# A hybrid decoder layer: later modulation moved from GpSimd to TensorE in four column strips, and the delta rule's heads taking turns

## The chip, the core and the metric

One Trainium2 chip, one core of it. A core has five engines that run at the same time and meet only through semaphores: TensorE (PE: matmuls; its weight loads are PEld), VectorE (DVE), ScalarE (ACT), GpSimd (POOL) and SyncE (SP). Each executes its own list of instructions in order. SP issues nearly all DMA transfers here, so a transfer that must wait for a buffer holds those behind it in SP's list. The metric is the device time of one execution in microseconds (us), as the median of several runs; less is better.

## What is computed

One decoder layer over 1,024 tokens of width 2,048, in float32. A conditioning vector c gives six modulation vectors; the tokens pass a mixer with four parallel head groups and then a mixture of experts, each with a DeepNorm residual:

```python
mod = (jax.nn.silu(c) @ w_ada[l] + b_ada[l]).astype(F32)
sh1, sc1, gt1, sh2, sc2, gt2 = jnp.split(mod, 6, axis=-1)
h = ada_input(x, sh1, sc1)
p = h @ w_in[l]
y_conv = short_conv_mixer(...)
y_rwkv = rwkv7_mixer(...)          # the delta rule, 8 heads of 64
y_att = swa_sink_attention(...)    # window 128, sinks, relative bias
y_ssm = s5_mixer(...)
y_mix = jnp.concatenate([...], axis=-1) @ w_out[l]
x = layer_norm(ALPHA * x + (1.0 + gt1) * y_mix, ln_g[l, 0], ln_b[l, 0])
h = ada_input(x, sh2, sc2)
y_moe = hierarchical_moe(h, ...)   # top-1 group, then top-2 of 8 experts
x = layer_norm(ALPHA * x + (1.0 + gt2) * y_moe, ln_g[l, 1], ln_b[l, 1])
```

The delta rule keeps a 64 x 64 state per head: `state = state * w + v k^T + (state a) b^T`, read out as `state r` at each token. The first two modulation vectors (sh1, sc1) are needed before anything else; the other four, 4 x 2,048 columns, only from the output projection on. They are the "later modulation": a product of a vector of 2,048 numbers with 2,048 x 8,192 weights, 64 MB that are read once.

## The kernel before

Stages, in order of time: the startup (layer norm of the first 512 tokens, sh1 and sc1, the first columns of the input projection); the mixers; the rest of the output projection with the router; the experts; the last layer norm.

**The mixers** are one program order made of two interleaved streams. The first is the chain of the mixers itself: for each half of 512 tokens four calls of `rw_core` (two heads each) and the attention, and after the first half the state-space part. This chain is long, with small steps on DVE, ACT and PE that wait for each other. The second stream, the fill (`fills`), is the large matmuls: the input projection unit by unit, then blocks `a` and `b` of the output projection. It is a Python generator that yields after each group of three matmuls (a product of 128 x 128 by 128 x 512, split into a high and a low part) the time that it is thought to take, `MM3` = 0.64. At places where the chain would leave PE waiting, it calls `hop(us)`, which pulls that many microseconds of fill. All PE instructions are kept in program order, so this decides PE's list. The lists of the other engines are ordered by the scheduler of the framework with a simulated time line. For each weight tile of the fill ACT makes the high part (L325) and DVE the low part (L326); both are read by PE a little later.

**Side work** stands in two lists, P and Q, of which `side()` takes one item each; `side` is called three times in `rw_core`, once per attention block and once per state-space group. P held the eight tables of the state-space part (POOL), and then 16 blocks of the later modulation, two items each. `mod_part` makes a block of 512 columns: 16 tiles of 128 x 512 are loaded into the ring `mw` of six buffers (L579), POOL multiplies each by its column of silu(c) (L580) and adds it to a running sum (L582), and `end` loads the bias, lets PE sum over the 128 partitions with a column of ones, adds the bias on DVE (L590) and writes the 512 numbers to `md_d` in device memory. The ring `mw` is also used by the tables, the convolution and the output blocks.

**`rw_core`** treats 512 tokens in 8 chunks of 64, for two heads at once (64 partitions each). A loop of 31 steps (`tv`, L758 and L759) inverts 32-row triangular blocks on DVE, with `hop(0.88)` in each step. Later `pa` multiplies the solved blocks of the even chunks (partitions 0 to 63) and of the odd ones (64 to 127), L812, into the two buffers of `rwB`, and L814 and L815 copy the results out. In the last loop each chunk has 8 matmuls: for head 0 and then for head 1 two into the output `py` and two into the new state `pS` (bank `rwS`); DVE scales `pS` into the state `St` (L841).

`bias_rows` (Q) loads the bucket table and multiplies it at once (bank `rwA`).

PSUM in this stage: four `acc` banks for the fill, one `rwA`, two `rwB`, one `rwS`.

Of the kernel before, what the change touches and what calls it, by code (L numbers as in the profile page):

```python
# [11 lines left out]
F32 = mybir.dt.float32  # L12
# [3 lines left out]
ALU = mybir.AluOpType  # L16
# [4 lines left out]
D = 2048  # L21
S = 1024
HT = 512
KT = D // 128
# [44 lines left out]
PT = {}  # L69
# [97 lines left out]
class K:  # L167
# [203 lines left out]
    def unit(s, ws, ui, half, nxt):  # L371

        u = UNITS[ui]
        s5 = u[0][0] == "s5"
        n = 4 if s5 else len(u)
        acc = [s.ps("acc") for _ in range(n)]
        k = 0
        while k < KT:
            hi, lo = next(ws)
            for kk in range(hi.shape[1]):  # L380
                hh, hl = s.hk(half, k)
                a = 0
                for j in range(n):
                    if s5:
                        sl = slice(128 * j, 128 * j + 128)
                        s.mm3(acc[j], (hh[:, sl], hl[:, sl]), (hi[:, kk], lo[:, kk]), k == 0, k == KT - 1)
                    else:
                        w = u[j][2]
                        s.mm3(acc[j][:w], (hi[:, kk, a:a + w], lo[:, kk, a:a + w]), (hh, hl), k == 0, k == KT - 1)
                        a += w  # L390
                    yield MM3
                k += 1
                s.turn(half, nxt, k)
        for j in range(n):
            if s5:
                t = s.ev()
                s.nc.scalar.copy(t, acc[j])
                r0 = HT * half + 128 * j
                s.nc.sync.dma_start(s.u_d[r0:r0 + 128], t)
            else:  # L400
                s.spill(u[j], acc[j], half)
# [168 lines left out]
            s.nbs += 1  # L570
        return rest

    def mod_part(s, ci):

        nc, io, E = s.nc, s.io, s.nc.gpsimd
        a = s.mt()
        for k in range(KT):
            w = s.mt()
            nc.sync.dma_start(w, io["w_ada"][128 * (KT * ci + k):128 * (KT * ci + k) + 128])  # L579
            E.tensor_tensor(w if k else a, w, s.cs[:, k:k + 1].to_broadcast([128, 512]), op=ALU.mult)  # L580
            if k:
                E.tensor_tensor(a, a, w, op=ALU.add)  # L582

        def end():
            o = D * 2 + 512 * ci
            b = s.ev()
            nc.sync.dma_start(b[0:1], io["b_ada"][0:1, o:o + 512])
            pm = s.ps("rwB")
            s.mm(pm[0:1], s.c["ones"][:, 0:1], a, start=True, stop=True)
            nc.vector.scalar_tensor_tensor(b[0:1], pm[0:1], 0.0 if ci // 4 == 1 else 1.0, b[0:1], op0=ALU.add, op1=ALU.add)  # L590
            nc.sync.dma_start(s.md_d[0:1, 512 * ci:512 * ci + 512], b[0:1])
        return end

    def mod(s, t, c0):

# [94 lines left out]
    def rw_core(s, u, follow):  # L690

        nc, c, V, E = s.nc, s.c, s.nc.vector, s.nc.gpsimd
# [52 lines left out]
        for ch in range(NCH):  # L745
            e = ch % 2
# [58 lines left out]
        s.hop(1.1)  # L805
        XA = s.t4().rearrange("p (e x t) -> p e x t", e=2, t=64)
        for g in range(NCH // 4):
            for e in range(2):
                pa = s.ps("rwB")
                for x in range(4):  # L810
                    ix = 4 * g + x
                    s.mm(pa[0:64, x * 128:x * 128 + 128], XT[64 * e:64 * e + 64, ix], G[64 * e:64 * e + 64, ix // 2, ix % 2], start=True, stop=True)  # L812
                pv = pa[0:64].rearrange("p (x a t) -> p x a t", x=4, a=2)
                nc.scalar.copy(XA[0:64, e, 4 * g:4 * g + 4], pv[:, :, 0])  # L814
                V.tensor_copy(WV[0:64, e, 4 * g:4 * g + 4], pv[:, :, 1])  # L815
        PT = s.t2().rearrange("p (c t) -> p c t", t=64)
# [12 lines left out]
        py = s.ps("rwA")  # L829
        St = s.St[hp]  # L830
        for ch in range(NCH):
            pS = s.ps("rwS", (128, 64))
            e = ch % 2
            for h in range(2):
                sl = slice(64 * h, 64 * h + 64)
                x = (ch // 2) * 2 + h
                s.mm(py[sl, ch * 64:ch * 64 + 64], WV[:, e, x], RB[:, e, x, 0:64], start=True, stop=False)
                s.mm(py[sl, ch * 64:ch * 64 + 64], St[sl], R[sl, ch], start=False, stop=True)
                s.mm(pS[sl], RB[:, e, x, 64:128], WV[:, e, x], start=True, stop=False)
                s.mm(pS[sl], PT[sl, ch], St[sl], start=False, stop=True)  # L840
            V.tensor_scalar(St, pS, DC[:, ch:ch + 1], None, op0=ALU.mult)  # L841
            s.step()
            s.hop(1.1)
# [57 lines left out]
    def bias_rows(s):  # L901
        nc = s.nc
        rb = s.ev()
        nc.sync.dma_start(rb[0:32, 0:8], s.io["rel_bias"])
        nc.gpsimd.memset(rb[32:33, 0:8], NEG)
        oh = s.ev()
        nc.sync.dma_start(oh[0:33, 0:384], s.io["oh"][0:33])
        pf = s.ps("rwA")
        s.mm(pf[0:8, 0:384], rb[0:33, 0:8], oh[0:33, 0:384], start=True, stop=True)
        f = s.ev()  # L910
        nc.vector.tensor_copy(f[0:8, 0:384], pf[0:8, 0:384])
        nc.sync.dma_start(s.F_d, f[0:8, 0:384])
        nc.sync.dma_start(s.F2_d, s.F_d[None].to_broadcast([128, 8, 384]))
# [418 lines left out]
    def startup_and_mix(s):  # L1332
# [6 lines left out]
        with tc.tile_pool(name="EV", bufs=1, side=s.R) as s.EV:  # L1339
            with tc.tile_pool(name="start", bufs=1, side=s.R) as P, tc.tile_pool(name="ps0", bufs=1, space=PSUM) as s.psum:  # L1340
                s.psb = {"acc": 6, "tp": 2}
                s.startup(P)
            s.np, s.n2, s.n4, s.n8 = 6, 9, 6, 2
            with tc.tile_pool(name="LO", bufs=1, side=s.R) as s.LO:
                mix = s.LO.tile([128, MIX.shape[1]], F32, name="mix")
                nc.sync.dma_start(mix, io["mix"])
                for k, (a, n) in MIX_AT.items():
                    s.c[k] = mix[:, a:a + n]
                with tc.tile_pool(name="s5p", bufs=1, side=s.R) as P5:
                    s.s5_params(P5, s.LO)  # L1350
                with tc.tile_pool(name="M", bufs=1, side=s.R) as s.M, tc.tile_pool(name="ps1", bufs=1, space=PSUM) as s.psum:
                    s.psb = {"acc": 4, "rwA": 1, "rwB": 2, "rwS": 1}
                    s.mixers()

    def mixers(s):
# [22 lines left out]
        for gb in range(8):  # L1378
            P.append(lambda gb=gb: (rests.pop(gb - 1)() if gb else 0, rests.update({gb: s.s5_tables(gb)})))
        P.append(lambda: rests.pop(7)())  # L1380
        for ci in range(16):
            P.append(lambda ci=ci: rests.update({"m": s.mod_part(ci)}))
            P.append(lambda: rests.pop("m")())
        for i in range(4, 8):
            Q.append(lambda i=i: rests.update({"n": s.norm_b(i)}))
            if i in (9,):
# [57 lines left out]
            s.side()  # L1444
        while s.fill:
            s.pump()
        while s.convs:
            s.conv(*s.convs.pop(0))
        s.pin = False
# [13 lines left out]
    def out_cols(s, ws, key, acc, js=range(4), nxt=None):  # L1463

        for k in range(KT):
# [7 lines left out]
                yield MM3  # L1473
            if nxt:
                s.turn(key, nxt, k + 1)

    def out_block(s, ws, key, n, nxt):

        nc, V = s.nc, s.nc.vector
        ns = slice(512 * n, 512 * n + 512)  # L1480
        g = s.mt()
        s.mod(g, 512 * n)
        acc = [s.ps("acc") for _ in range(4)]
# [675 lines left out]
```

## Time and profile before

| | |
|---|---|
| median of three runs | 3643.0 us (3624.75 to 3646.46) |
| the profiled execution | 3632.17 us, of which the profile's span is 3630.4 us |
| granted TensorE clock over the span | 0.93 of full speed |
| PE busy | 3157.3 us, 87% of the span |
| DVE / ACT / POOL busy | 2632.2 / 1601.3 / 1443.0 us |

By stage, from the span's start: the startup to about 130 us; the mixers, with the tables on POOL from about 200 to 630 us and the later modulation on POOL from about 630 to 1880 us; output projection and router to about 2210 us; the experts to about 3530 us; then the last layer norm.

Times of one kind of instruction are given as busy time (overlaps counted once) and as the mean of one in nanoseconds. Matmuls overlap in the pipeline, so what one costs is better read from the distance between starts than from its length. A matmul of full float32 shows as two records, one of the split products as one. The granted clock is a share of full speed, averaged over the stretch; the two levels are 1.2 and 2.4 GHz. The columns of a stretch are its bounds, its length, then for each engine its busy time and instructions.

### The profile page before, as it was taken

How to read it: one execution, taken by the hardware profiler on the slowest of the kernel's cores; microseconds unless marked ns; L12 is line 12 of the kernel's file. 1: busy time of each engine (PE TensorE's matmuls, PEld its weight loads, DVE VectorE, ACT ScalarE, POOL GpSimd, SP SyncE). 2: the span in 40 equal slices, each digit the busy share in tenths (PEclk: the TensorE clock that was granted, in tenths of full speed). 3: DMA queues.
4: the chain of work that ended last, by engine and by line, in shares of the span. 5: the costliest groups of instructions: out<-in, count | busy, mean ns of one | idle time of the engine just before them, and what ended most of it. 6: DMA issues, size and time to landing. Idle time of an engine off the chain costs nothing. (4 is left out here: it accounts for less than half of the span.)

```text
span 3630.4 us, 46775 instructions
## 1 busy us (share of the span) xinstructions
PE 3157.3 (87%) x15757; PEld 2330.7 (64%) x15757; DVE 2632.2 (73%) x3973; ACT 1601.3 (44%) x2316; POOL 1443.0 (40%) x1173
## 2 busy tenths in 40 slices
PE   6888989888998998998888876998998999999980
PEld 4666767655577676666657664776776766667750
DVE  2466758595576468678556987698797796896986
ACT  4332323222322332322323545576675675675751
POOL 0067574677787004444444542042142151340411
PEclk9999989899999999899999967999999999999995
DMA  9555444564787445545446657799798897997964
GB/s 360 190 161 154 127 144 149 166 197 144 221 262 221 143 115 168 166 144 161 149 143 233 209 216 284 250 367 355 261 395 322 290 388 276 328 389 259 370 248 186
DMA packets 345301, 844.94 MB, mean 233 GB/s; under 512 B 93251, under 2 KB 173164, under 8 KB 280908
## 3 DMA queue, kind: packets, MB, share of 16 engines
q1 hardware_dynamic: 336396, 808.11, 63.4%
q0 software_dynamic: 8640, 33.61, 3.7%
q8 instruction: 129, 2.11, 0.2%
q14 instruction: 136, 1.11, 0.1%
HBM read 754.72 MB, written 111.49 MB: 239 GB/s over the span
## 5 line engine op out<-in xcount | busy, mean ns | idle before, releaser
L1841 DVE TENSOR_TENSOR partl<-raw,parth 128x1024 fp32r<-128x1024 f32 x768 | 903.9, 1221 | 160.4 <-ACT parth L1840 158.2
L1840 ACT CAST parth<-raw 128x1024 fp32r<-128x1024 f32 x768 | 776.5, 1049 | 283.8 <-PE h L180 151.6
L326 DVE TENSOR_TENSOR wlo<-wraw,whi 128x512 fp32r<-128x512 f32 (+2 forms) x472 | 417.0, 888 | 291.3 <-ACT whi L325 281.5
L325 ACT CAST whi<-wraw 128x512 fp32r<-128x512 f32 (+2 forms) x472 | 283.0, 603 | 729.0 <-PE acc L180 613.2
L580 POOL TENSOR_TENSOR mw<-mw,cs 128x512 f32<-128x512 f32 x256 | 305.6, 1200 | 603.2 <-DMA mw<-in_w_ada 296.4
L1922 POOL DMA_INDIRECT sum_d<-yo,list x37 | 253.3, 6846 | 624.6 <-DVE yo L1920 582.2
L180 PE MATMUL h<-partl,xh 128*128 128x512 f32 x1184 | 479.5, 409 | 9.4 <-DVE partl L1841 8.1
L180 PE MATMUL h<-parth,xh 128*128 128x512 f32 x1184 | 456.3, 399 | 12.7 <-ACT parth L1840 12.7
L180 PE MATMUL acc<-hh,whi 128*128 128x512 f32 (+1 forms) x1056 | 447.5, 428 | 15.3 <-ACT hh L352 7.0
L180 PE MATMUL acc<-hh,wlo 128*128 128x512 f32 (+1 forms) x1056 | 424.9, 404 | 40.8 <-DVE wlo L326 40.7
L180 PE MATMUL acc<-hl,whi 128*128 128x512 f32 (+1 forms) x1056 | 423.0, 401 | 0.0
L582 POOL TENSOR_TENSOR mw<-mw 128x512 f32<-128x512 f32 x240 | 347.8, 1449 | 6.4
L180 PE MATMUL acc<-whi,hh 128*128 128x512 f32 x640 | 274.0, 447 | 32.5 <-DVE ev L1490 18.3
L180 PE MATMUL acc<-wlo,hh 128*128 128x512 f32 x640 | 269.4, 421 | 33.6 <-DVE wlo L326 32.2
L180 PEld LDWEIGHTS h<-partl,xh 128*128 128x128 f32 x1184 | 225.8, 191 | 93.8 <-DVE partl L1841 48.2
L180 PEld LDWEIGHTS acc<-hh,wlo 128*128 128x128 f32 (+1 forms) x1056 | 202.7, 192 | 98.2 <-DVE wlo L326 51.5
L180 PEld LDWEIGHTS h<-parth,xh 128*128 128x128 f32 x1184 | 225.7, 191 | 61.2 <-ACT parth L1840 18.4
L180 PE MATMUL acc<-whi,hl 128*128 128x512 f32 x640 | 264.4, 413 | 0.0
L180 PEld LDWEIGHTS acc<-hh,whi 128*128 128x128 f32 (+1 forms) x1056 | 202.4, 192 | 84.1 <-issue 24.1
L1940 POOL DMA_INDIRECT xg<-h_d,list x39 | 114.0, 2923 | 348.1 <-DMA list<-list_d 224.2
L180 PE MATMUL y<-parth,al 128*64 128x512 f32 (+1 forms) x592 | 233.5, 399 | 14.3 <-DVE al L1901 7.9
L180 PE MATMUL y<-partl,ah 128*64 128x512 f32 (+1 forms) x592 | 237.1, 401 | 9.2 <-DVE partl L1841 9.2
(441 smaller groups left out, 5337.6 us busy)
## 6 DMA issues: line engine op xcount, KB each, us to landing
raw<-in_moe_w SPq DMA_DIRECT2D x384, 1024.0 KB
mw<-in_w_ada SPq DMA_DIRECT2D x256, 256.0 KB
wraw<-in_w_in SPq DMA_DIRECT2D x240, 256.0 KB
wraw<-in_w_out SPq DMA_DIRECT2D x160, 256.0 KB
wa<-in_wa SPq DMA_DIRECT2D x32, 1024.0 KB
pT_d<-ev SPq DMA_DIRECT2D x62, 256.0 KB
t<-s_tab SPq DMA_DIRECT2D x24, 512.0 KB
s_tab<-mw SPq DMA_DIRECT2D x32, 256.0 KB
```

The costliest lines, as they stand in the source:

```text
L180: return s.pinned(s.nc.tensor.matmul(*a, **k))
L325: s.nc.scalar.copy(v(hi), v(raw))
L326: s.nc.vector.tensor_sub(v(lo), v(raw), v(hi).bitcast(F32))
L580: E.tensor_tensor(w if k else a, w, s.cs[:, k:k + 1].to_broadcast([128, 512]), op=ALU.mult)
L582: E.tensor_tensor(a, a, w, op=ALU.add)
L1840: nc.scalar.copy(hi, x)
L1841: nc.vector.tensor_sub(lo, x, hi.bitcast(F32))
L1922: nc.gpsimd.indirect_dma_start(out=s.sum_d, out_offset=bass.IndirectOffsetOnAxis(ap=lst[0:n, 0:1].bitcast(I32), axis=0), in_=o, in_offset= ...
L1940: nc.gpsimd.indirect_dma_start(out=s.xgs[x][0:n], out_offset=None, in_=s.h2_d, in_offset=bass.IndirectOffsetOnAxis(ap=l[0:n, 0:1].bitcast( ...
```

## The change

1. **Later modulation.** `mod_part` goes, and with it POOL's multiplications and additions and the products with a column of ones. `mod_parts` is a generator of 64 steps (16 blocks of 512 columns, four steps each). A step takes four weight tiles of 128 x 512 and cuts each into four pieces of 128 columns; piece j is multiplied by the same column of silu(c), repeated 32 times as the weights, into strip j of 32 partitions of `rwS[:, 128:256]`. Every fourth step adds the bias by four matmuls with one row. DVE collects each step's result from PSUM (`mdacc`), and after the fourth writes four rows of 128 to `md_d`. The loads of the next step, and the bias, are issued right after the matmuls of this one. `modstep` runs one step; `unit` and `out_cols` call it after each four k, as fill worth 0.9, and an output block first runs what it needs.
2. **The heads take turns.** In each chunk the new state comes first, and each of the four kinds of matmul is issued for head 0 and head 1 before the next kind.
3. **Even and odd solved blocks take turns** in `pa`; both results are copied out after a `hop(0.88)`.
4. **`bias_rows`** has a `hop(8.8)` between its loads and its matmul.
5. `rwS` is one tile for the whole stage: columns 0 to 63 for the state, 128 to 255 for the modulation.

```diff
@@ unit
                 s.turn(half, nxt, k)
+                if k % 4 == 0 and s.mdp:
+                    yield s.modstep()
@@
-    def mod_part(s, ci):
-        nc, io, E = s.nc, s.io, s.nc.gpsimd
-        a = s.mt()
-        for k in range(KT):
-            w = s.mt()
-            nc.sync.dma_start(w, io["w_ada"][128 * (KT * ci + k):128 * (KT * ci + k) + 128])
-            E.tensor_tensor(w if k else a, w, s.cs[:, k:k + 1].to_broadcast([128, 512]), op=ALU.mult)
-            if k:
-                E.tensor_tensor(a, a, w, op=ALU.add)
-        def end():
...
-            s.mm(pm[0:1], s.c["ones"][:, 0:1], a, start=True, stop=True)
...
+    def mod_parts(s):
+        nc, io = s.nc, s.io
+        jobs = [(ci, q) for ci in range(KT) for q in range(4)]
+        def load(ci, q):
+            ws = []
+            for k in range(4 * q, 4 * q + 4):
+                ws.append(s.mt())
+                nc.sync.dma_start(ws[-1], io["w_ada"][128 * (KT * ci + k):128 * (KT * ci + k) + 128])
+            if q == 3:
+                ws.append(s.ev())
+                nc.sync.dma_start(ws[-1][0:1], io["b_ada"][0:1, 2 * D + 512 * ci:2 * D + 512 * ci + 512])
+            return ws
+        ws = load(*jobs[0])
+        yield
+        pq, pm = s.rwS[:, 128:256], s.mdacc
+        for i, (ci, q) in enumerate(jobs):
+            for x, w in enumerate(ws):
+                k = 4 * q + x
+                for j in range(4):
+                    if k < KT:
+                        s.mm(pq[32 * j:32 * j + 32], s.cs[:, k:k + 1].to_broadcast([128, 32]), w[:, 128 * j:128 * j + 128], start=x == 0, stop=x == 3 and q < 3)
+                    else:
+                        s.mm(pq[32 * j:32 * j + 32], s.c["ones"][0:1, 0:32], w[0:1, 128 * j:128 * j + 128], start=False, stop=True)
+            if q == 0:
+                nc.vector.tensor_copy(pm, pq)
+            elif q < 3:
+                nc.vector.tensor_add(pm, pm, pq)
+            else:
+                t = ws[4][:, 0:128]
+                nc.vector.scalar_tensor_tensor(t, pm, 0.0 if ci // 4 == 1 else 1.0, pq, op0=ALU.add, op1=ALU.add)
+                for j in range(4):
+                    nc.sync.dma_start(s.md_d[0:1, 512 * ci + 128 * j:512 * ci + 128 * j + 128], t[32 * j:32 * j + 1])
+                s.nmd += 1
+            if i + 1 < len(jobs):
+                ws = load(*jobs[i + 1])
+            yield
+    def modstep(s):
+        if s.mdp and next(s.mdp, 0) == 0:
+            s.mdp = None
+        return 0.9
@@ rw_core
         for g in range(NCH // 4):
+            pas = [s.ps("rwB") for e in range(2)]
+            for x in range(4):
+                ix = 4 * g + x
+                for e in range(2):
+                    s.mm(pas[e][0:64, x * 128:x * 128 + 128], XT[64 * e:64 * e + 64, ix], G[64 * e:64 * e + 64, ix // 2, ix % 2], start=True, stop=True)
+            s.hop(0.88)
             for e in range(2):
-                pa = s.ps("rwB")
-                for x in range(4):
-                    ix = 4 * g + x
-                    s.mm(pa[0:64, x * 128:x * 128 + 128], XT[64 * e:64 * e + 64, ix], G[64 * e:64 * e + 64, ix // 2, ix % 2], start=True, stop=True)
...
-            pS = s.ps("rwS", (128, 64))
+            pS = s.rwS[:, 0:64]
             e = ch % 2
-            for h in range(2):
-                sl = slice(64 * h, 64 * h + 64)
-                x = (ch // 2) * 2 + h
+            hx = [(slice(64 * h, 64 * h + 64), (ch // 2) * 2 + h) for h in range(2)]
+            for sl, x in hx:
+                s.mm(pS[sl], RB[:, e, x, 64:128], WV[:, e, x], start=True, stop=False)
+            for sl, x in hx:
+                s.mm(pS[sl], PT[sl, ch], St[sl], start=False, stop=True)
+            for sl, x in hx:
                 s.mm(py[sl, ch * 64:ch * 64 + 64], WV[:, e, x], RB[:, e, x, 0:64], start=True, stop=False)
+            for sl, x in hx:
                 s.mm(py[sl, ch * 64:ch * 64 + 64], St[sl], R[sl, ch], start=False, stop=True)
-                s.mm(pS[sl], RB[:, e, x, 64:128], WV[:, e, x], start=True, stop=False)
-                s.mm(pS[sl], PT[sl, ch], St[sl], start=False, stop=True)
@@ bias_rows
+        s.hop(8.8)
         pf = s.ps("rwA")
@@ out_cols
+            if s.mdp and k % 4 == 3:
+                yield s.modstep()
@@ out_block
+        while s.nmd <= n:
+            yield s.modstep()
```

What this moves on PE, at two places. First the modulation. Before, PE's list has one matmul for a whole block of 512 columns (`mw` is POOL's sum, `per` the column of ones), between the state-space products:

```order
L180 MATMUL acc<-hh,whi 128x512
L180 MATMUL acc<-hl,whi 128x512
L180 MATMUL acc<-hh,wlo 128x512
L180 MATMUL rwB<-mw,per 1x512
L180 MATMUL rwA<-tp,t_8289 128x128
L180 MATMUL rwA<-t_8238,tp 128x128 x2
```

Now a step stands among the large matmuls of a unit of the input projection; the next step follows 24 of these later:

```order
L180 MATMUL acc<-wlo,hh 128x512
L180 MATMUL acc<-whi,hl 128x512
L180 MATMUL rwS<-mw,cs 32x128 x16
L180 MATMUL rwS<-ev,per 32x128 x4
L180 MATMUL acc<-whi,hh 128x512
L180 MATMUL acc<-wlo,hh 128x512
L180 MATMUL acc<-whi,hl 128x512
```

What was one matmul per block is now 64 + 4 in four groups, which read the weights themselves (`mw`, 512 columns in pieces of 128).

Second the first chunk of the delta rule in the third call of `rw_core` (`rwS` is the new state, `rwA` the output, `St` the state). Before:

```order
L180 MATMUL rwB<-t_5000,t_6012 64x128 x16
L180 MATMUL rwA<-t_5000,t_5001 64x64
L180 MATMUL rwA<-t_4824,St_1383 64x64
L180 MATMUL rwS<-t_5001,t_5000 64x64
L180 MATMUL rwS<-St_1383,t_6041 64x64
L180 MATMUL rwA<-t_5000,t_5001 64x64
L180 MATMUL rwA<-t_4824,St_1383 64x64
L180 MATMUL rwS<-t_5001,t_5000 64x64
L180 MATMUL rwS<-St_1383,t_6041 64x64
```

The first four are head 0, the last four head 1. Now:

```order
L180 MATMUL rwB<-t_5076,t_6054 64x128 x16
L180 MATMUL rwS<-t_5077,t_5076 64x64 x2
L180 MATMUL rwS<-St_1384,t_6092 64x64 x2
L180 MATMUL rwA<-t_5076,t_5077 64x64 x2
L180 MATMUL rwA<-t_4900,St_1384 64x64 x2
```

The same eight matmuls; each pair now goes to the two halves of the partitions.

## Rows read from the trace of the kernel before

**Rows 1.** Busy time in stretches: bounds, length, engines, clock, share of DMA, GB/s.

```profile
core 0: us, PE busy (x) PEld busy (x) DVE busy (x) ACT busy (x) POOL busy (x), PEclk, DMA share, GB/s
630.00:1880.00 1250.00, 1122.05 (x5789) 812.65 (x5788) 851.82 (x1373) 375.00 (x718) 643.71 (x500) 0.94 0.56 173
...
1180.00:1380.00 200.00, 196.76 (x998) 143.06 (x998) 105.41 (x215) 63.19 (x102) 0.00 (x0) 1.00 0.44 129
...
1400.10:1452.00 51.90, 39.84 (x151) 29.58 (x150) 49.91 (x88) 12.06 (x22) 28.28 (x23) 0.93 0.55 175
```

**Rows 2.** Groups of DVE, 960 to 1170 us, then 1200 to 1360: busy, mean ns.

```profile
L326 DVE TENSOR_TENSOR wlo<-wraw,whi 128x512 fp32r<-128x512 f32 x48 | 52.2, 1094 | 38.6 <-ACT whi L325 33.1 <-PE acc L180 2.0 <-PE rwB L183 2.0
...
L326 DVE TENSOR_TENSOR wlo<-wraw,whi 128x512 fp32r<-128x512 f32 x37 | 25.4, 687 | 26.3 <-ACT whi L325 26.1
```

**Rows 3.** Waits of PE: total us, times, longest; 630 to 1880, then 130 to 630.

```profile
PE acc L180 <- DVE wlo L326: 40.7, 27, 5.3
...
PE rwA L180 <- DMA ev<-in_oh: 9.1, 1, 9.1
```

**Rows 4.** Large matmuls (`acc`) in five solving loops: PE, PEld, DVE, ACT, clock.

```profile
764.60:815.30 50.70, 39.74 (x145) 28.69 (x146) 0.00 (x0) 2.23 (x4) 0.93 0.59 187
1278.20:1307.10 28.90, 27.73 (x119) 22.11 (x119) 0.00 (x0) 1.18 (x2) 1.00 0.49 144
1400.10:1452.00 51.90, 39.54 (x149) 29.20 (x148) 0.00 (x0) 1.18 (x2) 0.93 0.55 175
1543.90:1586.80 42.90, 36.61 (x145) 27.90 (x145) 2.73 (x4) 0.00 (x0) 0.96 0.48 159
1678.00:1717.90 39.90, 32.52 (x130) 23.67 (x130) 0.00 (x0) 0.00 (x0) 0.99 0.42 132
```

**Rows 5.** Groups of POOL, 630 to 1880 us: busy us, mean ns, idle before.

```profile
L582 POOL TENSOR_TENSOR mw<-mw 128x512 f32<-128x512 f32 x240 | 347.8, 1449 | 6.4
L580 POOL TENSOR_TENSOR mw<-mw,cs 128x512 f32<-128x512 f32 x256 | 305.6, 1200 | 603.2 <-DMA mw<-in_w_ada 296.4 <-DVE mw L893 220.6 <-DVE wlo L326 47.9
```

**Rows 6.** Timeline of PE in the startup: start, us, instruction.

```profile
62.17 0.39 PE L180 MATMUL acc<-hh,wlo 128*128 128x512 f32 x1
62.49 1.07 PE L180 MATMUL tp<-wa,csb 128*32 128x256 f32 x16
63.49 0.50 PE L180 MATMUL acc<-hh,whi 128*128 128x512 f32 x1
63.83 0.40 PE L180 MATMUL acc<-hl,whi 128*128 128x512 f32 x1
64.06 0.39 PE L180 MATMUL acc<-hh,wlo 128*128 128x512 f32 x1
```

**Rows 7.** Groups of PE by shape, whole span.

```profile
L180 PE MATMUL rwB<-t,t 64*64 64x128 f32 x512 | 51.3, 318 | 8.2 <-DVE t L815 6.2 <-DVE t L804 2.0
...
L180 PE MATMUL rwB<-mw,per 128*1 128x512 f32 x32 | 16.3, 590 | 1.8 <-DVE t L715 1.8
...
L180 PE MATMUL rwB<-t,t 64*64 64x64 f32 x256 | 9.6, 223 | 0.0
```

**Rows 8.** Timeline of PE: the solved blocks, the next product, the first chunk.

```profile
1754.82 1.58 PE L180 MATMUL rwB<-t,t 64*64 64x128 f32 x16 [0.44 <-DVE t L815]
1756.81 1.97 PE L180 MATMUL rwB<-t,t 64*64 64x128 f32 x32 [0.41 <-DVE t L815]
1758.70 0.33 PE L180 MATMUL rwA<-t,t 128*64 128x64 f32 x2
...
1760.76 0.50 PE L180 MATMUL acc<-whi,hh 128*128 128x512 f32 x1
```

**Rows 9.** Waits of POOL, 630 to 1880; timelines of SP and of POOL, one load.

```profile
POOL mw L580 <- DMA mw<-in_w_ada: 296.4, 98, 60.7
...
1415.08 0.38 SPq L579 DMA_DIRECT2D mw<-in_w_ada  x1
...
1417.93 1.11 POOL L580 TENSOR_TENSOR mw<-mw,cs 128x512 f32<-128x512 f32 x1 [3.85 <-DMA mw<-in_w_ada]
```

More of the change, by code (lines that the diff above doesn't have):

```diff
@@ L571, in norm_b @@
         return rest
-    def mod_part(s, ci):
-        nc, io, E = s.nc, s.io, s.nc.gpsimd
-        a = s.mt()
-        for k in range(KT):
-            w = s.mt()
-            nc.sync.dma_start(w, io["w_ada"][128 * (KT * ci + k):128 * (KT * ci + k) + 128])
-            E.tensor_tensor(w if k else a, w, s.cs[:, k:k + 1].to_broadcast([128, 512]), op=ALU.mult)
-            if k:
-                E.tensor_tensor(a, a, w, op=ALU.add)
-        def end():
[L585 to L588, printed above, removed]
-            s.mm(pm[0:1], s.c["ones"][:, 0:1], a, start=True, stop=True)
-            nc.vector.scalar_tensor_tensor(b[0:1], pm[0:1], 0.0 if ci // 4 == 1 else 1.0, b[0:1], op0=ALU.add, op1=ALU.add)
-            nc.sync.dma_start(s.md_d[0:1, 512 * ci:512 * ci + 512], b[0:1])
-        return end
+    def mod_parts(s):
[34 more added lines that the diff above has]
+            yield
@@ L807, in rw_core @@
         for g in range(NCH // 4):
-            for e in range(2):
-                pa = s.ps("rwB")
-                for x in range(4):
-                    ix = 4 * g + x
-                    s.mm(pa[0:64, x * 128:x * 128 + 128], XT[64 * e:64 * e + 64, ix], G[64 * e:64 * e + 64, ix // 2, ix % 2], start=True, stop=True)
-                pv = pa[0:64].rearrange("p (x a t) -> p x a t", x=4, a=2)
+            pas = [s.ps("rwB") for e in range(2)]
[4 more added lines that the diff above has]
+            s.hop(0.88)
+            for e in range(2):
+                pv = pas[e][0:64].rearrange("p (x a t) -> p x a t", x=4, a=2)
                 nc.scalar.copy(XA[0:64, e, 4 * g:4 * g + 4], pv[:, :, 0])
@@ L1352, in startup_and_mix @@
                     s.psb = {"acc": 4, "rwA": 1, "rwB": 2, "rwS": 1}
+                    s.rwS = s.ps("rwS")
                     s.mixers()
@@ L1380, in mixers @@
         P.append(lambda: rests.pop(7)())
-        for ci in range(16):
-            P.append(lambda ci=ci: rests.update({"m": s.mod_part(ci)}))
-            P.append(lambda: rests.pop("m")())
+        s.mdp, s.nmd = None, 0
+        s.mdacc = s.LO.tile([128, 128], F32, name="mdacc")
+        P.append(lambda: setattr(s, "mdp", s.mod_parts()))
         for i in range(4, 8):
@@ L1446, in mixers @@
             s.pump()
+        while s.mdp:
+            s.modstep()
         while s.convs:
@@ L1480, in out_block @@
         ns = slice(512 * n, 512 * n + 512)
+        while s.nmd <= n:
+            assert s.mdp
+            yield s.modstep()
         g = s.mt()
```

## The prediction

> **What bounds the kernel now.** I read the busy time by stretch first, then who TensorE (PE) waits for, then GpSimd (POOL), then single timelines. The stretch from 630 to 1880 us is the one in which POOL makes the later modulation. In it PE is busy 1122 of 1250 us, at a granted clock of 0.94 [rows 1]. So PE is the bound, and what can be won is either its work or its loss. I call loss the idle time plus what a low clock costs: 1250 - 1122 = 128 us idle, and 0.06 x 1250 = 75 us of clock, together 203 us.
>
> Inside that stretch lies an accident that acts as an experiment: from 1180 to 1380 us POOL does nothing, since its next block waits for a buffer. There PE is busy 196.8 of 200 us at clock 1.00 [rows 1], a loss of 3 us, 1.6%. The other 1050 us lose 200 us, 19%. What differs is VectorE (DVE). Its weight split at L326 takes 1094 ns while POOL is busy and 687 ns while POOL is quiet [rows 2], and the longest wait of PE is for just that split [rows 3]. The clearest case is the loop that solves the 32-row blocks (31 steps of two DVE instructions): with POOL quiet it lasts 28.9 us, with POOL at work 39.9 to 51.9 us, and PE, which has fill matmuls between the steps, waits in those [rows 1, 4].
>
> **The change, part by part.** The sum is made against the profiled execution's own 3632.2 us; the median of the three runs, 3643.0, lies 10.8 us above it.
>
> *POOL's multiplications and additions go.* 256 and 240 instructions, 305.6 and 347.8 us busy [rows 5]. They are on no path themselves; what counts is the DVE time that they cost. In the four slow solving loops PE runs 145, 149, 145 and 130 large matmuls [rows 4], at 0.23 us from one to the next [rows 6] 33.4, 34.3, 33.4 and 29.9 us of work, in 50.7, 51.9, 42.9 and 39.9 us: 54 us lost. The quiet loop, with 119, loses 28.9 - 27.4 = 1.5 us. So the loops should give back 54 - 6 = 48 us. Of the other 200 - 54 = 146 us I take 40%, 58 us, because not every wait there is for a slowed DVE instruction. Together -106. Lower bound 0 (the splits get faster and PE then waits for something else), upper bound 200 - 1.6% of 1050 = 183 (all of it becomes as quiet as 1180 to 1380).
>
> The Trainium skill (SBUF — State Buffer, the section on what contends at the ports) says that a DVE instruction with two SBUF inputs and a GpSimd instruction that reads SBUF exclude each other for the whole instruction. The trace agrees for the two-input split, 687 against 1094 ns. By that rule all of the excess would vanish, and the sum would go by the upper bound.
>
> *The old sums over the partitions go.* 16 products with a column of ones, 32 records, 16.3 us [rows 7]: -16.
>
> *The modulation comes to PE.* 64 steps of 16 matmuls of 128 columns into four strips of 32, and one in four has 4 small ones more for the bias. The startup has the same shape with 256 columns: 8 matmuls (16 records), the same 2048 columns as one step, stand between large matmuls. They take 63.49 - 62.49 = 1.00 us, and the neighbours' pitch grows from 0.23 to 0.32 and 0.34 [rows 6]: 1.00 + 0.09 + 0.11 = 1.20 us a step. 64 x 1.20 + 16 x 0.2 = +80. Best case 64 x 1.00 = 64. If pieces of half the width overlap only like two strips, at 62 ns a record [rows 8], the 2176 records cost 134. I take 80, the same columns in the same strips.
>
> *The loads of these weights now hold PE.* Before, only POOL waited for them: 296 us in 98 waits, 3.0 us each [rows 9]. After, a step's four loads are issued when the buffers of the step before come free, and SyncE's (SP's) queue has weight loads between them. One load went out at 1415.08 and POOL began with it at 1417.93, 2.85 us later [rows 9]. The order puts 24 large matmuls between two steps, 24 x 0.23 = 5.5 us at least. So most loads are there in time, but what waits behind them is everything on PE. I take 0.4 us a step, +25; bounds 0 and 64 x 3.0 = 192. DVE gets 64 reads of 128 columns from PSUM and loses 16 of 512, which the third of its time that is free (851.82 of 1250 us are busy) hides; if PE waited for one it would cost as much as a split.
>
> *The delta rule's chunks.* One chunk is 8 matmuls, 16 records, one head after the other, and the weights' shape changes at each matmul: 1760.76 - 1758.70 = 2.06 us [rows 8]. After, the heads alternate and the shape changes at every second one. Bounds: 2.06 (nothing gained) and 16 x 37.5 ns = 0.60, the pitch of the alternating 64 x 64 products (9.6 us for 256) [rows 7], which never change shape. A change of shape cost 0.09 and 0.11 us in the startup; four of them on top give 1.0, and with 62 ns a record [rows 8] 1.4. I take 1.2: 64 chunks x 0.86 = -55 (0 to -93).
>
> The Trainium skill (TensorEngine Tiling (Array Packing), Key Properties) says that changing the tiling mode drains the engine. That speaks against the 0.60: by that rule four drains a chunk stay. The trace agrees with its 0.09 and 0.11 us.
>
> *Even and odd solved blocks.* Now 8 records of one half, then 8 of the other: 1.58 us for 16, 99 ns a record; the product behind it, whose halves alternate, has 1.97 us for 32, 62 ns [rows 8]. 256 records x 37 ns = -9, and of the 6.2 us of PE waits for the copies behind them [rows 7] half: -12 in all. The new fill of 0.88 us hides the copies. Bounds 0 and -16.
>
> *The bias table.* PE waits 9.1 us once for its load [rows 3]; fill now stands there: -9, at worst 0.
>
> Sum: -106 - 16 + 80 + 25 - 55 - 12 - 9 = -93. 3632 - 93 = 3539 by the profiled execution, and 3643 - 93 = **3550** by the median.
>
> Where does the time go next? The steps lengthen the fill, so about 80 - 24 = 56 us more fill (the new hops use 24) is left when the second attention ends. It runs there alone at the full rate, so it is in the sum once already. Of the stages after it I change nothing: none of their instructions is touched.
>
> **The rivals.**
> - *All of the stretch becomes quiet* (upper bound, and the skill's rule). Another 77 us: 3473. For it: 1180 to 1380. Against it: that window has no output blocks, whose evacuations also hold PE.
> - *Strips are no cure for the chunks* (the change doesn't do what it says there). The order of the accumulations in one bank, not the strip, would set the 2.06 us: 55 back, 3605. Against it: the alternating products at 37.5 and 62 ns.
> - *DVE was not what held PE.* POOL's release gives nothing: 106 back, 3656, no change. For it: of the 203 us only some 41 are waits for the split by name [rows 3]. Against it: the loops.
> - *Slower: each step waits for its weights.* One mechanism, at the 64 steps in the queue behind SP's other loads: at POOL's 3.0 us a wait, 192 instead of 25, so 3717. It decides from (93 + 25) / 64 = 1.8 us a step on. For it: POOL's 98 waits with the same six buffers. Against it: POOL asked for a load each 3 us without a pause, and PE comes back only after 24 large matmuls.
>
> **How the numbers follow.** Chances: forecast 0.54, all quiet 0.11, chunks unchanged 0.11, DVE no matter 0.13, weights late 0.11. A measurement of this kernel tells about 1% from no change, 36 us. Faster by over that: the forecast, the quiet case, and most of the case of unchanged chunks (3605 lies at the border, 0.07), 0.72. Slower: weights late, 0.11. The rest, 0.17, is the same. The range reaches from the quiet case to past 3605: 3470 to 3630. Outside are weights late and most of the DVE case. The forecast's own range, from the middle bounds of its terms, is 3500 to 3600.
>
> **What would show it.** POOL empty from about 640 us to the row work; L326 near 690 ns after that; solving loops of about 30 us, four of them shorter; a chunk of 1.0 to 1.4 us; modulation groups on PE of about 1.0 us in 64 places and their waits for loads under 0.5 us on average; the clock of the stretch above 0.96. The forecast is wrong if PE waits over 1.8 us a step for weights, if the chunk stays near 2 us, or if the loss of the stretch stays near 19% though the splits are fast.

## The result, and the profile after

The changed kernel takes 3505.9 us (median of four runs, 3502.7 to 3513.8); the kernel before, run beside it, 3643.1 us. The ratio is 0.9636, with a 95% interval of 0.9601 to 0.9672: 133 us faster by the ratio, 137 by the medians. The forecast was 3550 us, 44 us too slow, with a range of 3470 to 3630. The profiled execution lasts 3502.7 us (span 3500.9), 129.5 us under that of before.

The busy time of the engines, from the page of the changed kernel (engine, busy us, share of the span, instructions):

```profile
PE 3100.5 (89%) x17901; PEld 2297.9 (66%) x17901; DVE 2423.5 (69%) x4021; ACT 1596.3 (46%) x2316; POOL 798.6 (23%) x677
```

POOL lost 644 us of work, and DVE 209 us though the change hands it 64 more reads of PSUM. Two stretches answer to [rows 1]: the later mixers, and the earlier ones, in which POOL still makes tables. Columns as there.

```profile
640.00:1800.00 1160.00, 1098.02 (x7958) 801.31 (x7958) 644.46 (x1421) 376.37 (x724) 0.63 (x2) 0.98 0.61 190
130.00:640.00 510.00, 447.31 (x2512) 347.67 (x2512) 354.37 (x789) 167.13 (x282) 284.04 (x501) 0.94 0.50 149
```

The same two of the kernel before, with the first drawn to the end of its own mixers:

```profile
640.00:1928.00 1288.00, 1149.19 (x5882) 830.45 (x5881) 858.47 (x1382) 382.73 (x732) 639.92 (x499) 0.94 0.55 171
```
```profile
130.00:640.00 510.00, 449.24 (x2441) 349.44 (x2440) 346.72 (x780) 164.06 (x274) 284.16 (x501) 0.93 0.49 146
```

Split the later stretch as the prediction did. Before, 1288 - 1149 = 139 us idle and 0.06 x 1288 = 77 us of clock, 216 us lost; what is left, 1072 us, is the work at full rate. After, 62 us idle and 0.02 x 1160 = 23 us of clock, 85 us lost, 1075 us of work. (The clock has two decimals, so such a loss is good to some 6 us.) PE does as much work in that stretch as before, and the whole gain, 131 us, is loss that went. In the earlier stretch nothing moved: 97 us lost before, 93 after.

The waits of PE from 640 to 1800 us (total, times, longest) answer to [rows 3] and to the modulation's new loads:

```profile
PE acc L180 <- DVE ev L1532: 17.1, 8, 3.9
...
PE acc L180 <- DVE wlo L326: 4.6, 7, 1.0
...
PE rwS L180 <- DMA mw<-in_w_ada: 3.4, 6, 1.0
...
PE rwS L180 <- DVE mdacc L605: 2.7, 2, 2.3
```

The wait for the split was 40.7 us and is 4.6. The 64 steps wait 3.4 us for their weights, all together. A step on PE and the neighbours that its shape slows, from the timeline (start, us, instruction):

```profile
715.80 0.39 PE L180 MATMUL acc<-wlo,hh 128*128 128x512 f32 x1
716.03 0.40 PE L180 MATMUL acc<-whi,hl 128*128 128x512 f32 x1
716.36 1.08 PE L180 MATMUL rwS<-mw,cs 128*32 128x128 f32 x32
717.37 1.12 PE L180 MATMUL rwA<-t,mix 128*128 128x512 f32 x2
```

717.37 - 716.36 = 1.01 us for the step, and 0.33 instead of 0.23 us ahead of it. A chunk of the delta rule, in the same view, answers to [rows 8]:

```profile
1614.77 0.34 PE L180 MATMUL rwS<-t,t 128*64 128x64 f32 x4
1615.04 0.33 PE L180 MATMUL rwS<-St,t 64*64 64x64 f32 x4
1615.30 0.34 PE L180 MATMUL rwA<-t,t 128*64 128x64 f32 x4
1615.56 0.33 PE L180 MATMUL rwA<-t,St 64*64 64x64 f32 x4
1615.82 0.50 PE L180 MATMUL acc<-whi,hh 128*128 128x512 f32 x1
```

1.05 us for 16 records, where it was 2.06: each run of four records of one shape takes 0.26 us. And the solving loops that answer to [rows 4], the large matmuls in each (PE, PEld, DVE, ACT, clock):

```profile
735.60:763.50 27.90, 22.28 (x90) 16.39 (x89) 0.00 (x0) 0.00 (x0) 1.00 0.46 142
1195.60:1223.70 28.10, 23.69 (x98) 17.82 (x97) 0.00 (x0) 1.18 (x2) 1.00 0.74 238
1308.30:1339.40 31.10, 25.62 (x104) 19.24 (x105) 0.00 (x0) 1.18 (x2) 1.00 0.84 279
1425.20:1468.80 43.60, 39.40 (x165) 30.79 (x166) 0.00 (x0) 1.64 (x3) 1.00 0.67 213
1552.20:1582.20 30.00, 27.91 (x120) 21.98 (x118) 0.81 (x2) 0.00 (x0) 1.00 0.30 100
```

Four are about as short as the one quiet loop of before (28.9 us). The fourth in the list lasts 43.6 us, but 165 matmuls, 38 us of work, lie in it; it is full, not waiting.

### The profile page after: what moved, and what is told of

It is laid out like the page before. It is cut to its first block, busy times and chain, and to the rows that moved or that the text cites. A ratio compares the mean times of both kernels' runs of the same rounds, so it can differ in the third digit from the quotient of the medians.

```text
span 3500.9 us, 50635 instructions
## 1 busy us (share of the span) xinstructions
PE 3100.5 (89%) x17901; PEld 2297.9 (66%) x17901; DVE 2423.5 (69%) x4021; ACT 1596.3 (46%) x2316; POOL 798.6 (23%) x677
## 3 DMA queue, kind: packets, MB, share of 16 engines
q8 instruction: 146, 2.39, 0.3%
## 5 line engine op out<-in xcount | busy, mean ns | idle before, releaser
L326 DVE TENSOR_TENSOR wlo<-wraw,whi 128x512 fp32r<-128x512 f32 (+2 forms) x472 | 354.4, 754 | 363.9 <-ACT whi L325 348.1
L180 PE MATMUL acc<-whi,hh 128*128 128x512 f32 x640 | 263.6, 431 | 24.2 <-DVE ev L1532 17.1
L180 PE MATMUL y<-parth,ah 128*64 128x512 f32 (+1 forms) x592 | 239.1, 405 | 5.3 <-ACT ah L1942 3.7
L180 PEld LDWEIGHTS acc<-hl,whi 128*128 128x128 f32 (+1 forms) x1056 | 202.2, 191 | 46.7 <-issue 9.8
```

Source lines behind the costliest of these rows:

```text
L180: return s.pinned(s.nc.tensor.matmul(*a, **k))
L326: s.nc.vector.tensor_sub(v(lo), v(raw), v(hi).bitcast(F32))
```

## Experiments

All ratios are to the kernel before, run beside the kernel in question. "Of the gain" means the difference of a ratio to 0.9636, times 3643 us; with the intervals such a difference is good to some 15 us.

**The two halves of the change, each alone.** The modulation on PE, with chunk, blocks and bias load as before:

```diff
 (changed kernel)
-            hx = [...]        # products of both heads in turn
+            for h in range(2): ...   # as before
-            pas = [s.ps("rwB") for e in range(2)] ...
+            for e in range(2): pa = s.ps("rwB") ...   # as before
-        s.hop(8.8)
```

> The changed kernel with the delta rule's chunk, the solved blocks and the bias load as before, so that of the change only the modulation on PE is left. Theory (the parts add up: POOL freed about -107, ones-products -16, 64 steps +82, their waits +4): 37 us under the kernel before, 3595 to 3625. Rival (the modulation's move brought nearly all of the 137 us and the turns next to nothing): 3510 to 3550.

Measured: 3587.3 us, ratio 0.9828 (0.9803 to 0.9852), 63 us under the kernel before; less than the rival asked, more than the theory. The stretch of its later mixers:

```profile
640.00:1896.00 1256.00, 1196.00 (x7997) 874.60 (x7996) 649.70 (x1425) 381.36 (x729) 0.63 (x2) 0.94 0.56 175
```

60 us idle and 0.06 x 1256 = 75 us of clock, 135 us lost: 81 less than before.

The other half, on the kernel before: the new order in chunk and blocks, the earlier bias load, the modulation still on POOL.

```diff
 (kernel before)
+            hx = [...]        # products of both heads in turn
+            pas = [s.ps("rwB") for e in range(2)] ...
+        s.hop(8.8)
```

> The kernel before with everything of the change but the modulation, which stays on POOL: the new order in the chunk and in the solved blocks, and the earlier bias load. Theory (PE is the bound and the parts add up: chunks -64, blocks -12 to -20, bias -9): 85 to 95 us under the kernel before, 3550 to 3570. Rival (with POOL at work PE waits for DVE right behind the shorter chunks, so that half of it is lost again): 35 to 50 us under it, 3595 to 3615.

Measured: 3617.7 us, ratio 0.9926 (0.9902 to 0.9949), only 27 us under it, less than both theories said. The stretch of its later mixers and two of its waits (PE from 640 to 1920 us):

```profile
640.00:1920.00 1280.00, 1084.81 (x5810) 775.15 (x5809) 862.91 (x1374) 376.77 (x724) 648.81 (x500) 0.92 0.56 171
```
```profile
PE acc L180 <- DVE wlo L326: 42.1, 28, 5.0
PE rwB L180 <- POOL mw L582: 26.5, 2, 19.3
```

Here 195 us are idle and 0.08 x 1280 = 102 us are clock: 297 us lost and 983 us of work. Against before the work fell by 89 us, about what the theory counts, and the loss rose by 81, of which 56 are idle time. PE became faster and then waited, but hardly where the rival looked for it. Added up by what ended them, PE's waits for DVE rose only from 108 to 117 us, and those for the splits not at all; 26.5 us are new waits for POOL itself, and waits for ACT rose from 28 to 44 us. POOL ended its modulation at 1869 us (before: 1876), though PE was faster. So the two halves alone bring 63 + 27 = 90 us, and together 133: the turns pay in full only with the modulation gone from POOL. How much of their lost gain is POOL's own pace, and how much is slowed DVE and ACT work, these runs don't separate. (The 81 less and the 81 more are a coincidence.)

**The chunk alone, back to its old order.**

```diff
 (changed kernel)
-            for sl, x in hx:
-                s.mm(pS[sl], RB[:, e, x, 64:128], WV[:, e, x], start=True, stop=False)
-            ...
+            for h in range(2):
+                ...           # py, py, pS, pS of one head, then of the other
```

> The changed kernel with only the order inside the delta rule's chunk as before (one head's four products after the other's). Theory (the change of the weights' shape at every product cost the chunk 2.06 us instead of 1.05, and all of it lies on PE, which is the bound): 64 x 1.0 = 64 us back, 3560 to 3580. Rival (the shorter chunk only makes PE wait elsewhere for the DVE instruction behind it, so that it gained little): 3506 to 3530.

Measured: 3550.6 us (3542.2 to 3563.5), ratio 0.9715 (0.9698 to 0.9733): 29 us of the gain by the ratios, 45 by the medians, between what the rival and the theory asked. The profiled execution is the slowest of the four, 61 us over that of the changed kernel; its chunks take 2.06 us again in the median, and its later mixers are

```profile
640.00:1864.00 1224.00, 1169.30 (x8005) 852.75 (x8004) 656.82 (x1443) 380.01 (x730) 0.92 (x5) 0.97 0.58 181
```

that is 55 + 37 = 92 us lost, 1132 of work. So 57 of the chunks' 65 us of work come back there, at a nearly unchanged loss (92 and 85 us). The other three runs are 10 to 21 us shorter, and nothing shows where; the size lies between 29 and 61 us.

**The solved blocks.** First both edits there undone (turns, and copies behind both halves and a fill):

```diff
 (changed kernel)
-            pas = [s.ps("rwB") for e in range(2)]
-            ...
-            s.hop(0.88)
             for e in range(2):
+                pa = s.ps("rwB")
+                ...           # four products of this half, then its copies
```

> The changed kernel with only the products behind the solved blocks as before: one half's four, their copies, then the other's, without the fill between. Theory (PE is the bound: 256 records at 99 instead of some 70 ns, and the waits for the copies, 8.2 instead of 1.6 us): 15 to 25 us more, 3520 to 3530. Rival (the fill that now stands ahead of the copies only moves the wait): 3500 to 3512.

Measured: 3541.1 us, ratio 0.9710 (0.9682 to 0.9738): 27 us of the gain, 35 by the medians, and more than the theory (15 to 25) or the rival allowed. Then the turns alone undone:

```diff
 (changed kernel)
-            for x in range(4):
-                ix = 4 * g + x
-                for e in range(2):
+            for e in range(2):
+                for x in range(4):
+                    ix = 4 * g + x
```

> The changed kernel with one of the two edits at the solved blocks undone: the four products of the even half come first and then the four of the odd half, so that they no longer take turns, but both still stand ahead of the copies and the fill of 0.88 us. Theory (the 27 to 35 us that came back with both edits undone were half the turns, 14 us of PE's time and what the clock adds, half the fill and the order ahead of the copies): 14 to 20 us more, 3518 to 3528. Rival A (all of it is the turns): 3530 to 3545. Rival B (all of it is the copies behind which PE waits, and the low clock that such waits leave behind): 3503 to 3515.

Measured: 3505.3 us, ratio 0.9632 (0.9609 to 0.9655): nothing, as its rival B said. The groups of these products, 130 to 1900 us (busy, mean ns, idle before), with turns and old copies undone, with the turns alone undone, and in the changed kernel:

```profile
L180 PE MATMUL rwB<-t,t 64*64 64x128 f32 x512 | 50.6, 312 | 6.0 <-DVE t L843 4.5 <-DVE t L832 1.4
```
```profile
L180 PE MATMUL rwB<-t,t 64*64 64x128 f32 x512 | 42.1, 277 | 0.8 <-DVE t L845 0.8
```
```profile
L180 PE MATMUL rwB<-t,t 64*64 64x128 f32 x512 | 36.7, 280 | 1.6 <-DVE t L845 1.6
```

The turns save 5.4 us of busy time and no time. What counts is that the copies no longer stand between the products, or the fill ahead of them, which these two runs don't tell apart. With both edits undone the later mixers are

```profile
640.00:1842.00 1202.00, 1124.19 (x7958) 823.21 (x7957) 644.70 (x1421) 378.93 (x724) 0.63 (x2) 0.95 0.59 183
```

so 78 us idle and 0.05 x 1202 = 60 us of clock, 138 us lost, as with the modulation alone (135), where the changed kernel loses 85. The group itself has only 4 us more of waits; the larger part shows in the clock. One place of the kernel with both edits undone, in stretches and as a timeline of PE:

```profile
1596.00:1612.00 16.00, 16.00 (x98) 12.37 (x96) 12.69 (x24) 3.58 (x6) 0.00 (x0) 1.00 0.52 128
1612.00:1616.00 4.00, 0.04 (x3) 0.00 (x0) 0.18 (x1) 0.00 (x0) 0.00 (x0) 1.00 0.94 253
1616.00:1640.00 24.00, 22.75 (x146) 17.64 (x146) 7.92 (x17) 2.70 (x6) 0.00 (x0) 0.51 0.29 107
```
```profile
1611.33 0.71 PE L180 MATMUL rwB<-t,t 32*32 32x32 f32 x32
1617.24 0.79 PE L180 MATMUL acc<-whi,hh 128*128 128x512 f32 x1 [5.20 <-DVE ev L1530]
1617.84 0.63 PE L180 MATMUL acc<-wlo,hh 128*128 128x512 f32 x1
1618.26 0.63 PE L180 MATMUL acc<-whi,hl 128*128 128x512 f32 x1
```

A wait of 5.2 us is followed by 24 us at 1.2 GHz with PE busy, which cost 12 us beside the wait itself: matmuls go at 0.42 instead of 0.23 us. That is 12 of the 37 us of clock that this version loses more than the changed kernel. The wait is for an output block's evacuation by DVE, not for the solved blocks; why the old order of the copies brings it about there stays open.

**The strips in sequence.** The 16 matmuls of a step, the same ones, strip after strip:

```diff
 (changed kernel)
-            for x, w in enumerate(ws):
-                for j in range(4):
+            for j in range(4):
+                for x in range(4):
                     s.mm(pq[32 * j:32 * j + 32], ...)
```

> The changed kernel with the 16 matmuls of a modulation step in another order: the four of one strip after each other, then the next strip, instead of strip after strip in turns. The same matmuls, sums and loads. Theory (what makes 16 matmuls of 128 columns take 1.0 us is that neighbours lie in different strips and run beside each other): a step takes 2 to 4 us, so 64 x 1 to 3 = 64 to 190 us more, 3570 to 3700. Rival (the order doesn't matter, a matmul takes its time by its columns alone): 3500 to 3515, a step 1.0 us.

Measured: 3567.7 us, ratio 0.9789 (0.9770 to 0.9807), 56 us of the gain, just under the theory's range. The step in the timeline, and the stretch of its later mixers:

```profile
706.77 2.46 PE L180 MATMUL rwS<-mw,cs 128*32 128x128 f32 x32
709.16 0.50 PE L180 MATMUL acc<-whi,hh 128*128 128x512 f32 x1
```
```profile
640.00:1867.00 1227.00, 1181.74 (x7965) 889.43 (x7964) 650.58 (x1425) 378.50 (x725) 0.72 (x3) 0.99 0.58 180
```

2.39 instead of 1.01 us: neighbours in different strips overlap far more than neighbours in one strip. 64 x 1.38 = 88 us more work, of which 56 arrive: the loss is down to 45 + 12 = 57 us. That the longer steps fill waits is likely, but not tested.

**Does POOL slow DVE, and by what?** Three times the changed kernel with work that nobody needs on POOL behind each of the 64 steps; nothing is left out. Two inputs in SBUF:

```diff
 (changed kernel, behind each step)
+            nc.vector.tensor_copy(s.tick[:, i % 16:i % 16 + 1], pm[:, 0:1])
+            for x in range(4):
+                nc.gpsimd.tensor_tensor(s.idle, s.mix[:, 0:448], <tick column>, op=ALU.mult)
+                nc.gpsimd.tensor_tensor(s.idle, s.idle, s.mix[:, 0:448], op=ALU.add)
```

> The changed kernel with idle work put back on GpSimd (POOL): behind each of the 64 modulation steps POOL multiplies a tile of 448 columns by a column that VectorE (DVE) has just written and adds it to the tile, four times over, 8 instructions with two SBUF inputs, 512 in all (the kernel before had 496 of 512 columns). Nothing reads what they make, no load or buffer hangs on them, and TensorE's (PE's) work is the same. Theory (POOL's work slows DVE's splits and copies, and PE waits for those): most of the 132 us of loss that went from the stretch comes back, 80 to 130 us, so 3585 to 3635; the weight split at L326 goes from near 690 ns to 1000 ns or more between 700 and 1360 us, and the solving loops there from 28 to 31 us to 40 us or more. Rival (the gain came from something else that went with the old modulation: its buffers, its place in SP's queue, the products with the ones): 3500 to 3520, whatever the splits do.

Writes only:

```diff
 (in place of the four pairs)
+            nc.gpsimd.tensor_copy(s.idle[:, 0:1], <tick column>)
+            for x in range(16):
+                nc.gpsimd.memset(s.idle, 0.0)
```

> The changed kernel with POOL kept busy in another way: behind each of the 64 modulation steps it copies one column that DVE has written and then fills a private tile of 448 columns with zeros 16 times, 1024 instructions that write SBUF and read nothing. Nothing reads the tile. Theory (POOL instructions that read SBUF are what DVE contends with): 3500 to 3520 and L326 near 690 ns between 700 and 1360 us. Rival (any POOL access to SBUF slows DVE): back by as large a share as POOL is busy, 3550 to 3630, with L326 at 900 ns or more.

One large input:

```diff
 (in place of the four pairs)
+            for x in range(8):
+                nc.gpsimd.tensor_scalar(s.idle, s.mix[:, 0:448], <tick column>, None, op0=ALU.mult)
```

> The changed kernel with POOL kept busy behind each of the 64 modulation steps by 8 multiplications of a tile of 448 columns by a column, into a private tile that nothing reads: one large SBUF input each, where the earlier experiment with idle POOL work had two. Theory (any POOL instruction that reads SBUF takes turns with DVE's two-input ones): L326 at 900 ns or more between 700 and 1360 us and 3550 to 3610 us. Rival (only POOL instructions with two inputs do): L326 near 690 ns and 3500 to 3520.

Measured: two inputs 3598.6 us, ratio 0.9853 (0.9832 to 0.9874); writes 3509.8, 0.9616 (0.9600 to 0.9632); one input 3553.1, 0.9744 (0.9722 to 0.9765). Groups of DVE, 705 to 1362 us (busy, mean ns), of the changed kernel:

```profile
L326 DVE TENSOR_TENSOR wlo<-wraw,whi 128x512 fp32r<-128x512 f32 x128 | 88.0, 688 | 143.3 <-ACT whi L325 130.9 <-DMA wraw<-in_w_in 3.1 <-PE rwB L183 3.1
...
L1005 DVE TENSOR_REDUCE sm<-t 128x4 f32<-128x1024 f32 x6 | 7.1, 1206 | 0.0
...
L1017 DVE TENSOR_SCALAR t<-t,sm 128x256 f32<-128x256 f32 x24 | 6.7, 347 | 0.1
```

With POOL instructions of two inputs:

```profile
L326 DVE TENSOR_TENSOR wlo<-wraw,whi 128x512 fp32r<-128x512 f32 x111 | 121.2, 1098 | 77.9 <-ACT whi L325 77.4
...
L1021 DVE TENSOR_SCALAR t<-t,sm 128x256 f32<-128x256 f32 x24 | 20.7, 927 | 0.1
...
L1009 DVE TENSOR_REDUCE sm<-t 128x4 f32<-128x1024 f32 x6 | 7.1, 1205 | 0.0
```

With POOL instructions that only write:

```profile
L326 DVE TENSOR_TENSOR wlo<-wraw,whi 128x512 fp32r<-128x512 f32 x128 | 87.9, 688 | 132.9 <-ACT whi L325 126.3 <-PE rwB L183 3.1 <-DMA pT_d<-ev 1.3
L1021 DVE TENSOR_SCALAR t<-t,sm 128x256 f32<-128x256 f32 x24 | 12.4, 579 | 0.1
...
L1009 DVE TENSOR_REDUCE sm<-t 128x4 f32<-128x1024 f32 x6 | 7.1, 1205 | 0.0
```

With one large input:

```profile
L326 DVE TENSOR_TENSOR wlo<-wraw,whi 128x512 fp32r<-128x512 f32 x120 | 90.4, 755 | 118.3 <-ACT whi L325 110.5 <-PE rwB L183 3.1 <-DMA wraw<-in_w_in 3.1
```

Work of two inputs, on which nothing hangs, gives back 79 us (89 against the run with writes, made beside it), and the stretch, which lost 85 us in the changed kernel and 216 before, now loses 182:

```profile
640.00:1899.00 1259.00, 1139.84 (x7967) 826.67 (x7966) 826.75 (x1486) 376.73 (x725) 602.23 (x514) 0.95 0.56 175
```

It had 512 instructions of 448 columns, where the old modulation had 496 of 512; by columns, 79 to 89 us become 87 to 99. That is an estimate of the share that POOL's contention has in the gain, and no more, since the waits are not all those of the kernel before. Two of PE from 640 to 1380 us:

```profile
PE rwS L180 <- DVE mdacc L605: 13.4, 6, 5.5
PE rwS L180 <- DMA mw<-in_w_ada: 9.1, 13, 2.2
```

Both stand at the modulation's own steps, which the kernel before did not have on PE. Over the whole stretch the two kinds take 32 us, against 6 in the changed kernel, while the idle time grew by 57. 1024 POOL instructions that only write, busy 487 us, cost nothing that can be measured.

The Trainium skill (SBUF — State Buffer, Who interferes with whom) says that a two-input DVE instruction contends with GpSimd instructions that read SBUF and not with ones that only write. The trace agrees: 1098 and 688 ns, and the one-input reduction keeps its 1205 ns in both. POOL work with one large input falls between theory and rival, 755 ns and 39 us of the gain. The longest split there takes 1097 ns, though a POOL instruction takes 1407 and most splits overlap one. If the two excluded each other for the whole instruction, as the prediction took it, splits that start inside such an instruction would often take longer than that, so here the measurement decides.

**A version that beats both.** The same reasoning for the stretch that the change left as it was: the tables of 200 to 640 us on DVE.

```diff
     def s5_tables(s, gb):
-        E = nc.gpsimd
+        E = nc.vector
```

> The changed kernel with the tables that POOL makes between 200 and 640 us (8 blocks, 284 us of POOL) made by DVE instead; it could beat both kernels. Theory (POOL's work is what costs PE there: 63 us idle and some 31 us of clock between 130 and 640 us): DVE's splits get fast there as they did behind it, DVE has room (354 of 510 us busy, less with fast splits, and POOL's work takes it perhaps 120 us), so 30 to 70 us go: 3435 to 3475. Rival (the table instructions stand in DVE's order ahead of splits and copies that PE waits for, and take away what the faster splits give): 3490 to 3540.

Measured: 3463.3 us, ratio 0.9494 (0.9475 to 0.9513), 52 us under the changed kernel. From 130 to 640 us:

```profile
130.00:640.00 510.00, 475.79 (x2755) 371.49 (x2747) 419.96 (x1288) 181.52 (x307) 3.64 (x37) 0.95 0.56 167
```

PE is busy 476 instead of 447 us; DVE took over 284 us of POOL's work and is busy only 66 us more. The same table instructions take DVE (first line, this version) half the time that they took POOL (second, changed kernel), and DVE's own splits fall from 845 ns (third, changed kernel) to 690 (fourth, this version):

```profile
L1188 DVE TENSOR_TENSOR mw<-mw 128x512 f32<-128x512 f32 x32 | 22.1, 691 | 0.3
```
```profile
L1188 POOL TENSOR_TENSOR mw<-mw 128x512 f32<-128x512 f32 x32 | 47.9, 1496 | 2.1
```
```profile
L326 DVE TENSOR_TENSOR wlo<-wraw,whi 128x512 fp32r<-128x512 f32 x97 | 81.7, 845 | 56.7 <-ACT whi L325 56.6
```
```profile
L326 DVE TENSOR_TENSOR wlo<-wraw,whi 128x512 fp32r<-128x512 f32 x107 | 73.8, 690 | 16.4 <-ACT whi L325 15.9
```

Then the rows ahead of the router too:

```diff
-                E2 = V if i == 7 else nc.gpsimd
-                E = V if i >= 4 else nc.gpsimd
+                E2 = V
+                E = V
```

> The changed kernel with the tables of 200 to 640 us made by DVE, as in the experiment before, and with the scale, the offset and the second offset of the rows ahead of the router on DVE too, 72 additions and multiplications of 128 x 512 that POOL makes in 1.4 to 1.7 us each. Theory (what held for the tables holds for the rows: POOL is slower at them than DVE and slows DVE meanwhile; the longest wait of PE there is 12.9 us for POOL): 10 to 30 us under the version with only the tables moved, 3430 to 3455. Rival (the rows stage is DVE's own bound, 228 of 280 us busy, so that 72 more instructions at 0.69 us lengthen it): 3465 to 3500.

Measured: 3447.1 us, ratio 0.9450 (0.9422 to 0.9478), 16 us further by both; both intervals together allow 0 to 33, so this last step is not clear of noise. By its median it is the fastest version of this case, 5.5% under the kernel before.

## Why the prediction was right, and where it was off

- **PE is the bound; work and loss are what can be won.** Right: every run above is read by that split, and the work terms came out: together they are +3 us in the stretch.
- **POOL freed, -106, and waits for the weights, +25.** Together -81 of loss, and the modulation alone changed the loss by just that (216 to 135). That they meet is luck, since within the sum both are smaller than I had them: POOL's work put back costs an estimated 87 to 99 us by columns, and the loads wait 3.4 us in all, not 25, with 24 large matmuls between two steps as cover. The 40% that I took of the loss outside the solving loops was a guess, and no run tests it by itself. The rival of the slow loads had no ground, and the one in which DVE doesn't matter fell with POOL's work put back.
- **The terms add up.** This step failed. The turns alone, with POOL at work, turned 89 us of saved work into 81 us of new loss, so that the halves bring 90 us apart and 133 together. No term of the sum says what PE waits for once it is faster; there it was for POOL itself (26.5 us) and ACT (16 us more) rather than for DVE (8 us more).
- **Bound from above, 183, and the quiet rival, 3473.** Not reached: 7% of the stretch is still lost where the quiet window lost 1.6%. What was held against it shows: 17.1 us of waits for the output blocks' evacuation at L1532.
- **Ones-products, -16, and 64 steps, +80.** A step is 1.01 us (1.36 with the bias), its neighbours 0.32 and 0.34: 64 x 1.20 + 16 x 0.35 = 82 us, by the medians of the changed kernel.
- **Chunks, -55 by 1.2 us.** Measured 1.05, so 64 x 1.0 = 65 us of work, and 29 to 61 us of time when undone. The rival that the strips are no cure fell.
- **Solved blocks, -12 (0 to -16).** The term that was mis-sized most. The turns, which made 9 of the 12, save 5.4 us of busy time and no time that can be measured; the copies and the fill bring 27 to 35 us, by a loss of 85 instead of 138. I had priced the copies by the 6.2 us of waits in their own group, and not by the low clock, which is where most of it lay (60 against 23 us).
- **Bias table, -9.** The wait is gone from the list of 130 to 640 us, but the loss of that stretch stayed (97 and 93 us), so the gain there is not seen by itself.

In sum the forecast was 44 us too high. Taken one by one, 22 us are waits for weights that did not come, 15 to 23 the solved blocks, up to 10 the chunks; POOL's term, 7 to 19 too large, goes the other way. As the terms don't add up, this is an account of sizes and not a proof.

## What to carry to other kernels

Read a stretch as work plus loss, and ask of each saving of work what PE will wait for next: with the modulation still on POOL, saved work came back as loss (89 us saved, 27 seen). GpSimd instructions with two SBUF inputs beside a busy VectorE are dear even off every path (79 to 89 us for work that nobody reads); try them on VectorE, where they took half the time here and its own splits became faster. In column strips, put neighbours in different strips (1.01 against 2.39 us). Put the copies of a group of products behind all of them, with fill ahead of the copies (27 to 35 us here).

## What the runs showed of the hardware that I had not expected

- How much POOL slows DVE depends on both instructions. A one-input float32 multiplication by a column takes 347 ns alone, 579 beside POOL writes and 927 beside POOL work with two inputs; the reduction over 1024 columns and the two-input split beside writes do not move (1205 and 688 ns). The Trainium skill (SBUF — State Buffer, Who interferes with whom) lists such a multiplication among the forms that can take both ports and contend with any GpSimd instruction; the 579 ns agree.
- Behind one wait of 5.2 us PE ran at half clock for 24 us, and was busy 95% of them.
